# Feed-forward of a one-core DeltaNet layer: windows of 1024 tokens, and w_out in a stage of its own through DRAM

## The chip, the cores and the metric

The kernel runs on one core of a Trainium2 chip. The metric is the device time of one execution in microseconds, as the median of three runs. One further execution, the profiled one, left the trace from which all rows below are read.

## What is computed

One layer: a bidirectional gated DeltaNet mixer over 256 context and 2048 latent tokens of 1024 channels, then a gated feed-forward, then a norm. All inputs are float32. The change touches the feed-forward and what hands over to it:

```python
x_lat = x_lat + mod_l[2] * y_lat
h_lat = modulate(rms_norm(x_lat, norm2_g[i]), mod_l[3], mod_l[4])
x_lat = x_lat + mod_l[5] * conv_glu(h_lat, ...)
return rms_norm(x_lat, final_norm_g)

def conv_glu(h, w_in, conv_w, conv_b, w_out):       # 2 x 2816 inner channels
    val, gate = jnp.split(h @ w_in, 2, axis=-1)
    gate = dw_conv(gate, conv_w) + conv_b           # 3 taps along the tokens
    return (val * jax.nn.silu(gate)) @ w_out
```

## The kernel before

The program has two phases, whose operations (`Op`s of a `Plan`) are put into an order by a list schedule with rough costs and priorities: mixer first (projections, matrices, scans), then `plan2` (the output projection of the mixer, tile by tile of 128 tokens in `OUT_ORDER`, giving `x1_d` and the normed and transposed `h2_d` in DRAM) and `plan3` (the feed-forward). All transfers are issued on SP's queue, in order.

Every product is done in three matmuls, because a float32 operand is carried as two parts, `hi` and `lo`, that float32r holds: hi·hi, hi·lo, lo·hi (`mm3`, L832 to 836). Making the parts is a step of its own (`form`): ScalarE casts `hi` (L1752), VectorE or GpSimd subtracts it to get `lo` (L1755).

`plan3` works on four windows of 512 tokens (`WINDOWS`). In each, 11 groups follow one another; a group is two times 128 inner channels. Of a group the gate's product and the value's product are each a two by two block product: channels by halves of the contraction by halves of the window's tokens (256, for the gate 258 with a halo). `products3` takes seven products instead of eight (Winograd's), so that sums of blocks of the weights (`raw`, L1834, on GpSimd), of the tokens (`braw`, L1789, on VectorE, once a window) and of the results (`pc`, L1885; `zg`, L1931; `val`, L1962, on VectorE out of PSUM) take the place of the eighth. One product is four times `mm3`: 12 matmuls, with tile name `fps`, stationary `wf`, moving `bf`. Four PSUM banks (tags `zp` and `tr`, two each) hold the products in turn. Then come the taps of the convolution (`facc`, L1948, two on VectorE), SiLU, the product with the value and the parts of the hidden channels (`hid`, GpSimd L1970 and L1978).

The same group is at once multiplied with its 256 rows of `w_out`: the rows are loaded, split (`w`, L2000 and L2003, the latter on VectorE), 48 matmuls of 512 columns (`fy`) make the part of the output of four token tiles, and VectorE adds each half tile out of PSUM to a running sum in SBUF (`ya`, L2027). After the last group the sum is scaled, added to `x1`, normed and stored (`final`, L2050 to L2058; for the last window `rescale` and `finish`, L2072 to L2104).

So `w_in` (22 MB) and `w_out` (11 MB) are read and split once for each of the four windows, 44 groups in all. In the program's order on PE each group is 168 `fps` matmuls and 48 `fy` matmuls.

## Time and profile before

| | us |
|---|---|
| median of 3 runs | 3507.01 (3506.76 to 3510.5) |
| profiled execution, first to last instruction (its span, the only time recorded of it) | 3517.0 |
| PE busy in the span | 3302.4 (94%) |
| VectorE busy | 3017.5 (86%) |
| GpSimd busy | 2533.5 (72%) |
| ScalarE busy | 2016.5 (57%) |

PE is the matmul side of TensorE, PEld its weight loads, DVE VectorE, ACT ScalarE, POOL GpSimd, SP the queue of the transfers. The feed-forward begins at about 2000 us and runs to the end. A matmul's own duration contains the time through the array and overlaps the next one; what a matmul costs in a row of them is the step from one start to the next.

### The profile page before, as it was taken

How to read it: one execution, taken by the hardware profiler on the slowest of the kernel's cores; microseconds unless marked ns; L12 is line 12 of the kernel's file. 1: busy time of each engine (PE TensorE's matmuls, PEld its weight loads, DVE VectorE, ACT ScalarE, POOL GpSimd, SP SyncE). 2: the span in 40 equal slices, each digit the busy share in tenths (PEclk: the TensorE clock that was granted, in tenths of full speed). 3: DMA queues.
4: the chain of work that ended last, by engine and by line, in shares of the span. 5: the costliest groups of instructions: out<-in, count | busy, mean ns of one | idle time of the engine just before them, and what ended most of it. 6: DMA issues, size and time to landing. Idle time of an engine off the chain costs nothing.

```text
span 3517.0 us, 74716 instructions
## 1 busy us (share of the span) xinstructions
PE 3302.4 (94%) x27594; PEld 3027.7 (86%) x27594; DVE 3017.5 (86%) x5574; ACT 2016.5 (57%) x5265; POOL 2533.5 (72%) x2630
## 2 busy tenths in 40 slices
PE   7979999999999999999999889998999899988998
PEld 4969899999899989999977789987899789977997
DVE  6678788888898898886565699999999999999998
ACT  6548666666677777776355454444444444444443
POOL 5347677676777787776555587778887888778876
PEclk8989999999999999999999999999999999999999
DMA  7321132232323232322566533333333333324232
GB/s 247 124 68 54 39 98 78 81 97 75 107 75 96 71 105 68 84 60 77 175 197 199 168 104 106 104 107 126 97 108 97 125 110 101 108 72 146 93 104 90
DMA packets 198309, 373.18 MB, mean 106 GB/s; under 512 B 18865, under 2 KB 103081, under 8 KB 196920
## 3 DMA queue, kind: packets, MB, share of 16 engines
q1 hardware_dynamic: 197944, 368.41, 34.2%
q8 instruction: 217, 3.56, 0.4%
q14 instruction: 148, 1.21, 0.1%
HBM read 316.36 MB, written 51.98 MB: 105 GB/s over the span
## 4 chain that ended last, share of the span: by engine, by line
PE 59%; DVE 22%; issue 6%; POOL 6%; ACT 4%; DMA 3%; SPq 0%; DVEq 0%; ACTq 0%; POOLq 0%
PE zps L834 6%; PE fps L834 5%; PE fps L836 5%; PE fps L835 5%; PE zps L835 5%; PE zps L836 5%; PE fy L834 3%; DVE acc L891 3%; PE fy L835 3%; PE fy L836 3%; PE scps L1248 3%; POOL raw L1834 3%; DVE wf L1755 2%; PE scps L1266 2%; PE scps L1275 2%
## 5 line engine op out<-in xcount | busy, mean ns | idle before, releaser
L834 PE MATMUL fps<-bf,wf 128*128 128x258 f32 (+1 forms) x2464 | 708.5, 288 | 61.6 <-DVE val L1962 27.2
L834 PE MATMUL zps<-hhl,wt 128*128 128x260 f32 (+1 forms) x2176 | 697.5, 321 | 10.5 <-DVE acc L891 6.3
L836 PE MATMUL fps<-bf,wf 128*128 128x258 f32 (+1 forms) x2464 | 701.5, 285 | 1.3 <-DVE wf L1755 1.1
L835 PE MATMUL fps<-bf,wf 128*128 128x258 f32 (+1 forms) x2464 | 701.9, 285 | 0.0
L835 PE MATMUL zps<-hhl,wt 128*128 128x260 f32 (+1 forms) x2176 | 619.4, 285 | 1.9 <-POOL hhl L962 1.9
L836 PE MATMUL zps<-hhl,wt 128*128 128x260 f32 (+1 forms) x2176 | 618.8, 284 | 0.0
L962 POOL TENSOR_TENSOR hhl<-hraw,hhl 128x260 fp32r<-128x260 f32 x568 | 427.7, 774 | 155.0 <-ACT hhl L958 152.7
L834 PEld LDWEIGHTS fps<-bf,wf 128*128 128x128 f32 x2464 | 473.1, 192 | 75.7 <-DVE val L1962 27.8
L1752 ACT CAST wf<-raw 128x512 fp32r<-128x512 f32 x616 | 360.4, 619 | 305.1 <-POOL raw L1834 147.3
L1755 DVE TENSOR_TENSOR wf<-raw,wf 128x512 fp32r<-128x512 f32 x440 | 498.3, 1144 | 26.3 <-ACT wf L1752 24.5
L835 PEld LDWEIGHTS fps<-bf,wf 128*128 128x128 f32 x2464 | 473.4, 192 | 1.7
L836 PEld LDWEIGHTS fps<-bf,wf 128*128 128x128 f32 x2464 | 472.8, 192 | 2.1 <-DVE wf L1755 2.1
L891 DVE SCALAR_TENSOR_TENSOR acc<-zps,convw,acc 128x256 f32<-128x256 f32 x832 | 398.8, 480 | 60.5 <-ACT acc L889 44.7
L834 PEld LDWEIGHTS zps<-hhl,wt 128*128 128x128 f32 x2176 | 417.6, 192 | 19.7 <-issue 10.5
L835 PEld LDWEIGHTS zps<-hhl,wt 128*128 128x128 f32 x2176 | 418.3, 192 | 2.4 <-POOL hhl L962 2.3
L836 PEld LDWEIGHTS zps<-hhl,wt 128*128 128x128 f32 x2176 | 414.9, 191 | 0.1
L1834 POOL TENSOR_TENSOR raw<-raw 128x512 f32<-128x512 f32 x176 | 288.0, 1636 | 160.9 <-DVE wf L1755 145.0
L1152 POOL TENSOR_TENSOR ct<-U,cst_lm 128x256 f16<-128x256 f16 x432 | 303.5, 724 | 66.6 <-PE inv L1159 54.3
L1182 ACT CAST yz<-inv 128x256 f16<-128x256 f32 x864 | 275.4, 380 | 85.9 <-PE inv L1176 83.4
L1755 POOL TENSOR_TENSOR wf<-raw,wf 128x512 fp32r<-128x512 f32 x176 | 268.7, 1545 | 76.2 <-ACT wf L1752 75.4
L834 PE MATMUL fy<-w,hid 128*128 128x512 f32 x704 | 282.0, 401 | 30.3 <-DVE ya L2027 27.8
L1834 POOL TENSOR_TENSOR raw<-raw,raw 128x512 f32<-128x512 f32 x176 | 278.6, 1583 | 12.6
(258 smaller groups left out, 8929.7 us busy)
## 6 DMA issues: line engine op xcount, KB each, us to landing
raw<-in_ffn_in SPq DMA_DIRECT2D x176, 512.0 KB
hraw<-hT_d SPq DMA_DIRECT2D x284, 260.0 KB
raw<-in_ffn_out SPq DMA_DIRECT2D x88, 512.0 KB
wmx<-in_w_mod SPq DMA_DIRECT2D x128, 128.0 KB
wt_st<-in_w_qkv SPq DMA_DIRECT2D x24, 512.0 KB
hT_d<-hb SPq DMA_DIRECT2D x36, 260.0 KB
wm<-in_w_mod SPq DMA_DIRECT2D x8, 1024.0 KB
xt<-in_x SPq DMA_DIRECT2D x16, 512.0 KB
```

Of the source, the lines that this page charges most:

```text
L834: mm(out, lh, rh, start=first, stop=False)
L835: mm(out, lh, rl, start=False, stop=False)
L836: mm(out, ll, rh, start=False, stop=last)
L891: nc.vector.scalar_tensor_tensor(acc.t, ps.t[:, k:k + TB], wk, acc.t, ALU.mult, ALU.add)
L962: nc.gpsimd.tensor_tensor(t[:, 1, k], raw[q].t[:, k], t[:, 0, k].bitcast(F32), ALU.subtract)
L1152: nc.gpsimd.tensor_tensor(col_sets(ct, lb, LATE), col_sets(U.t[:, 0], lb, LATE), v3(self.lm[:, li]), ALU.mult)
L1182: nc.scalar.copy(col_sets(yz.t[:, k], lb, sets), v3(ps.t[:, k]))
L1248: nc.tensor.matmul(ps.t[:, k, :], blk.t[:, ci, k, :], S.t, start=True, stop=True)
L1266: nc.tensor.matmul(ps.t[:, 2, :], pz.t[:, ci, 0, :], r.t if S is not None else blk.t[:, ci, 3, :], start=True, stop=True)
L1752: nc.scalar.copy(f.t[:, 0], src())
L1755: (nc.vector if eng == "DVE" else nc.gpsimd).tensor_tensor(f.t[:, 1], src(), f.t[:, 0].bitcast(F32), ALU.subtract)
L1834: return pl.op("POOL", 1.25, lambda: nc.gpsimd.tensor_tensor(part(*out), part(*a), part(*b), op), deps, prio, uses=[raw[k] for k in {out[0 ...
```

## The change

- **Two stages.** `ffn_window` now runs over two windows of 1024 tokens and ends with the hidden channels, unsplit, in DRAM (`hid_d`). `ffn_out` follows: for each half of the 1024 output columns and each block of 512 tokens (the last two blocks 256) it loads the hidden channels, splits them, and sums all 22 times 128 channels in PSUM, in one bank for each token tile, on two sets of four banks in turn.
- **Wider products.** The halves of a window's tokens are 512, so an `fps` matmul has 512 columns, and there are no halos: the convolution runs over the window, and three columns are carried to the next (`carry`).
- **Sums of token blocks through DRAM.** `combine` makes T1 to T4 and stores them in `comb_d`; `tokens` loads blocks and sums in halves of the contraction and splits them. For the second window `combine` runs during the first.
- **Who splits.** All `lo` parts of `w_in` are VectorE's (before, two of seven were GpSimd's). The `lo` parts of the hidden channels move from GpSimd to VectorE and are made twice, once for each half of the columns; those of `w_out` are made once instead of four times, half of them on GpSimd. The `ya` sums are gone; in their place stand, once, a scaling out of PSUM and a sum (`half_out`, `finish_out`), with the first half of the rows kept in `y_d`.
- `OUT_ORDER` has the blocks of the first 1024 tokens before the last three.

What operations there are (built program): `fps` matmuls 7392 before, 3696 now; `fy` 2112 and 2112. On VectorE `wf` 440 of 512 columns before, 462 of 512 and 44 of 256 now (308 for `w_in`, the rest hidden channels), `w` 176 to 10 of 1024 columns (now `bf<-raw`), `ya` 320 to none, results out of PSUM 616 of 256 or 258 to 308 of 512. On GpSimd `raw` 352 to 176, `wf` 176 and `hid` 88 to none.

Core of the diff (removed comments and what follows from the new tile names left out):

```diff
-HT = TB + 2
+WB = 512
...
-OUT_ORDER = [4, 5, 3, 6, 2, 1, 7, 8]
+OUT_ORDER = [4, 5, 3, 2, 1, 6, 7, 8]
...
-WINDOWS = [1, 0, 2, 3]
-FIRST_SLOTS = {"bf": 7, "raw3": 2, "wf": 1}
+SLOTS3 = {
+    "braw": (4, 0, 0), "bf": (5, 7, 2), "raw3": (2, 0, 2), "wf": (4, 0, 3), "pc": (0, 3, 0), "big3": (0, 2, 4), "st3": (0, 0, 4),
+}
...
+    def combine(self, w, prio):
...
+            def less(k, r, a, b, deps, p=p, bufs=bufs):
+                x = pl.op("DVE", 1.15, lambda: nc.vector.tensor_tensor(
+                    bufs[r].t, bufs[a].t, bufs[b].t, ALU.subtract), deps, prio, uses=[bufs[x] for x in {r, a, b}])
+                s = self.comb_done[k, p] = pl.op("SP", 1.5, lambda: nc.sync.dma_start(
+                    self.comb_d[w][k][:, 2 * p:2 * p + 2, :], bufs[r].t), [x], prio, uses=[bufs[r]])
+                return x, s
+            l = [load(0, 0, 0), load(1, 0, 1), load(2, 1, 1), load(3, 1, 0)]
+            t1, s1 = less(0, 0, 1, 0, l[:2])
+            t3, _ = less(2, 1, 2, 1, [t1, l[2]])
+            t2, _ = less(1, 0, 2, 0, [t3, s1])
+            less(3, 3, 3, 0, [t2, l[3]])
+        self.combine(w, prio - (0 if w == 0 else 900))
+        done = dict(self.comb_done)
+        def form(src, deps, eng):
+            r = Buf("braw")
...
+        def block(q, j, eng="DVE"):
+            blk = 2 * w + j
+            deps = [self.h2_done[4 * blk + c] for c in range(4)]
+            return [form(self.h2_d[blk][:, 4 * q + 2 * p:4 * q + 2 * p + 2, :], deps, eng) for p in range(2)]
...
+        b11, b21, t1, t2 = block(0, 0), block(1, 0), comb(0, "POOL"), comb(1)
+        t3, b22, t4 = comb(2, "POOL"), block(1, 1), comb(3)
+        return b11, b21, b22, t4, t1, t2, t3
...
+        f3 = form(1, 0, [s3], "DVE")
-        f4 = form(0, 1, [s4], "POOL")
-        f3 = form(1, 0, [s3], "POOL")
+        f4 = form(0, 1, [s4], "DVE")
...
+            def mms(p):
+                if p == 0:
+                    acc.t = self.pp.tile([P, WB], F32, name="fps", tag=acc.tag, bufs=2)
+                for k in range(2):
+                    kk = 2 * p + k
                     self.mm3(
-                        cols(acc), w.t[:, 0, k, :], w.t[:, 1, k, :], x.t[:, 0, k, toks], x.t[:, 1, k, toks], k == 0, k == 3
+                        acc.t, w.t[:, 0, kk, :], w.t[:, 1, kk, :], x[p].t[:, 0, k, :], x[p].t[:, 1, k, :], kk == 0, kk == 3
                     )
-            acc.done = pl.op(
-                "PE", 12 * (n + 8) / 2400, mms, [w.done, x.done, self.last_out], prio, alloc=[acc], uses=[w, x]
-            )
+            a = self.last_prod
+            for p in range(2):
+                a = pl.op(
+                    "PE", 1.37, lambda p=p: mms(p), [w.done, x[p].done, self.last_out, a], prio,
+                    alloc=[acc] if p == 0 else [], uses=[w, x[p]] + [acc] * p,
+                )
+            acc.done = self.last_prod = a
             return acc
...
-    def ffn_window(self, k, w):
+    def ffn_window(self, w):
+        N = 2 * WB
...
+        n = N + 1 if w else N - 1
+        t0 = N - 1 if w else 0
...
+                def times(f=f):
+                    nc.gpsimd.tensor_tensor(v_[f].t[:, :n], v_[f].t[:, :n], a_[f].t[:, :n], ALU.mult)
+                def store(f=f):
+                    nc.sync.dma_start(self.hid_d[g][:, f, t0:t0 + n], v_[f].t[:, :n])
+                e = pl.op("POOL", 0.1, ends, vals[f], prio, uses=[v_[f]])
+                a = pl.op("POOL", 2.4, times, [e, acts[f]], prio, uses=[v_[f], a_[f]])
+                self.hid_done.setdefault(w, []).append(pl.op("SP", 1.5, store, [a], prio, uses=[v_[f]]))
+        for g in range(NF // 2):
+            hidden(g, base + 20 * g)
...
-                    hid.t = self.pools3[2].tile([P, 2, 2 * TB], F32R, name="hid", bufs=self.NHID)
-                    nc.scalar.copy(hid.t[:, 0], v_[f].t)
...
-                w2.done = pl.op("DVE", 0.61, lambda w2=w2, part=part: TT(
-                    w2.t[:, 1], part(), w2.t[:, 0].bitcast(F32), ALU.subtract), [a], prio, uses=[st, w2])
...
-                    TT(accs[t].t[:, ns], ps.t, accs[t].t[:, ns], ALU.add)
...
-        ng = NF // 2
-        for g in range(ng + 1):
...
+    def ffn_out(self):
...
+        for half in range(2):
+            ns = slice(half * WB, (half + 1) * WB)
+            W = []
+            blocks = [[0, 1, 2, 3], [4, 5, 6, 7], [8, 9, 10, 11]] + ([[12, 13], [14, 15]] if half else [[12, 13, 14, 15]])
+            for i, ts in enumerate(blocks):
+                prio = base + 1000 * half + 100 * i
+                t0, nt = ts[0] * P, len(ts)
+                ps = [Buf((("inv", "inv", "sc", "sc"), ("zp", "zp", "tr", "tr"))[n_acc % 2][t]) for t in range(nt)]
+                n_acc += 1
+                a = None
+                for j in range(nj):
+                    p = prio + j - 25
+                    if i == 0:
+                        raw, l = self.load3(
+                            "raw3", [P, 2, WB], self.i["ffn_out"][2 * j:2 * j + 2, :, ns].rearrange("f p c -> p f c"), [], p
+                        )
+                        W.append(self.form(lambda raw=raw: raw.t, [2, WB], raw, [l], p, "bf", "DVE" if j % 2 else "POOL"))
+                    deps = self.hid_done[0] + (self.hid_done[1] if t0 + nt * P > 2 * WB - 1 else [])
+                    raw, l = self.load3("raw3", [P, 2, nt * P], self.hid_d[j][:, :, t0:t0 + nt * P], deps, p)
+                    hids = [
+                        self.form(lambda raw=raw, f=f: raw.t[:, f], [nt * P], raw, [l], p, "wf", "DVE") for f in range(2)
+                    ]
...
+                    for f in range(2):
+                        first = j == 0 and f == 0
+                        a = pl.op(
+                            "PE", 0.684 * nt, lambda f=f, mms=mms: mms(f), [a, W[j].done, hids[f].done], prio + j,
+                            alloc=ps if first else [], uses=[W[j], hids[f]] + ([] if first else ps),
+                        )
...
+                for t, c in enumerate(ts):
+                    if half == 0:
+                        y_done[c] = self.half_out(prio + 20, c, ps[t], a, near, m5, m5_done)
+                    else:
+                        self.finish_out(prio + 20, c, ps[t], a, near, m5, fg, junk, [m5_done, fg_done, new_junk], y_done[c], i > 2)
...
+    def half_out(self, prio, c, ps, done, near, m5, m5_done):
...
+        a = pl.op("DVE", 0.67, lambda: nc.vector.tensor_tensor(
+            row.t[:, :WB], ps.t, m5.t[:, :WB], ALU.mult), [l, done, m5_done], prio, uses=[row, ps, m5])
+        a = pl.op("POOL", 1.25, lambda: nc.gpsimd.tensor_tensor(
+            row.t[:, :WB], row.t[:, :WB], row.t[:, WB:], ALU.add), [a], prio, uses=[row])
...
+    def finish_out(self, prio, c, ps, done, near, m5, fg, junk, ready, y_done, late):
...
+        eng, add = ("DVE", nc.vector) if late else ("POOL", nc.gpsimd)
...
+        a = pl.op("DVE", 0.67, scaled, [done, *ready], prio, alloc=[tmp], uses=[ps, m5])
+        a = pl.op(eng, 0.61 if late else 1.25, lambda: add.tensor_tensor(
+            row.t[:, WB:], row.t[:, WB:], tmp.t, ALU.add), [a, l], prio, uses=[row, tmp])
+        s1 = pl.op("ACT", 0.6, lambda: square(1), [a, s0], prio, uses=[row, junk, st])
...
+        for k in range(2):
+            s = slice(k * WB, (k + 1) * WB)
+            a = pl.op("DVE", 0.67, lambda s=s: nc.vector.scalar_tensor_tensor(
+                row.t[:, s], row.t[:, s], st.t[:, 2:3], fg.t[:, s], ALU.mult, ALU.mult), [r], prio, uses=[st, row, fg])
+            pl.op("SP", 0.8, lambda s=s: nc.sync.dma_start(self.o[c * P:(c + 1) * P, s], row.t[:, s]), [a], prio, uses=[row])
```

PE, where products and `fy` meet. Before, in the middle of a window; `fps` has 256 columns, and the next group's products come 48 `fy` later:

```order
L834 MATMUL fps<-bf_37086,wf_38099 128x256
L835 MATMUL fps<-bf_37086,wf_38099 128x256
L836 MATMUL fps<-bf_37086,wf_38099 128x256
L834 MATMUL fy<-w_37991,hid 128x512
L835 MATMUL fy<-w_37991,hid 128x512
L836 MATMUL fy<-w_37991,hid 128x512
```

The change, at the only place where they meet (`wf` is then a split of hidden channels, `bf` one of `w_out`):

```order
L839 MATMUL fps<-bf_36593,wf_39501 128x512
L840 MATMUL fps<-bf_36593,wf_39501 128x512
L841 MATMUL fps<-bf_36593,wf_39501 128x512
L839 MATMUL fy<-bf_39594,wf_39625 128x512
L840 MATMUL fy<-bf_39594,wf_39625 128x512
L841 MATMUL fy<-bf_39594,wf_39625 128x512
```

The `fy` have moved from 44 places to the end: all 3696 `fps` stand in front of all 2112 `fy`, and only the output projection's last transposes stand among the first `fps`.

VectorE, from the value's products of a group to the next group, before (`raw` is the float32 load, `wf` its split, `pc` and `val` results out of PSUM, `w` splits of `w_out`, `ya` the running sums):

```order
L1962 TENSOR_TENSOR val<-fps,pc 128x256 x2
L1755 TENSOR_TENSOR wf_44595<-raw_44382,wf_44595 128x512
L1755 TENSOR_TENSOR wf_44597<-raw_44382,wf_44597 128x512
L1962 TENSOR_TENSOR val<-fps,pc 128x256
L1755 TENSOR_TENSOR wf_44611<-raw_44420,wf_44611 128x512
L2027 TENSOR_TENSOR ya<-fy,ya 128x512 x4
L2003 TENSOR_TENSOR w_44656<-raw_44443,w_44656 128x512
L2003 TENSOR_TENSOR w_44659<-raw_44601,w_44659 128x512
L2027 TENSOR_TENSOR ya<-fy,ya 128x512 x4
```

The change, over one set of seven products of the first window (`big` takes the results):

```order
L1957 TENSOR_TENSOR big_36115<-fps,pc_36095 128x512
L1755 TENSOR_TENSOR wf_36124<-raw_35930,wf_36124 128x512
L1904 TENSOR_TENSOR pc_36142<-fps,pc_36095 128x512
L1904 TENSOR_TENSOR pc_36146<-fps,pc_36142 128x512
L1755 TENSOR_TENSOR wf_36144<-raw_35930,wf_36144 128x512
L1904 TENSOR_TENSOR pc_36166<-fps,pc_36142 128x512
L1957 TENSOR_TENSOR big_36168<-fps,pc_36166 128x512
L1755 TENSOR_TENSOR wf_36164<-raw_35908,wf_36164 128x512
L1957 TENSOR_TENSOR big_36115<-fps,pc_36146 128x512
```

The `w` splits and `ya` sums are gone from between the products; at most one split stands between two results, and each piece is twice as wide against twice the columns of a product.

SP, from the last tiles of the output projection on (`x_d` and `h_d` are that projection's stores), before:

```order
L1776 DMA braw<-h_d_70 128x4x256
L1550 DMA x_32924<-in_x 128x1024
L1675 DMA h_d_75<-h_32938 1024x1x128
L1633 DMA x_d_98<-x_32796 128x1024
L1550 DMA x_33023<-in_x 128x1024
L1675 DMA h_d_75<-h_33036 1024x1x128
L1633 DMA x_d_99<-x_32924 128x1024
```

The change, at the same place:

```order
L1821 DMA braw_33077<-h_d_69 128x1024
L1674 DMA h_d_72<-h_33061 1024x1x128
L1821 DMA braw_33092<-h_d_69 128x1024
L1821 DMA braw_33106<-h_d_69 128x1024
L1635 DMA x_d_130<-x_32928 128x1024
L1821 DMA braw_33136<-comb_d_84 128x1024
L1821 DMA braw_33151<-comb_d_84 128x1024
L1821 DMA braw_33169<-comb_d_85 128x1024
```

From the `h2_d` store that completes the first window to the last token part, 30 transfers of 512 KB (8 loads and 8 stores of `combine`, 14 loads of `tokens`) stand among the projection's own, where 4 stood before.

## Rows read from the trace of the kernel before

**Rows 1.** Page part 2, the span in 40 slices (digits: tenths busy).
```profile
PE   7979999999999999999999889998999899988998
DVE  6678788888898898886565699999999999999998
```

**Rows 2.** Stretches: busy us (xcount) of PE, PEld, DVE, ACT, POOL; clock, DMA.
```profile
2300.00:2500.00 200.00, 175.93 (x1155) 160.54 (x1154) 189.43 (x225) 92.74 (x161) 162.36 (x101) 0.95 0.37 117
2900.00:3100.00 200.00, 200.00 (x1410) 187.81 (x1408) 190.22 (x258) 97.91 (x167) 157.11 (x101) 1.00 0.35 104
2000.00:3517.00 1517.00, 1412.18 (x9513) 1299.90 (x9511) 1444.76 (x1823) 713.40 (x1241) 1211.10 (x768) 0.98 0.34 107
```

**Rows 3.** PE's waits, 2000 to 3517 us: total, times, longest.
```profile
PE fy L834 <- DVE ya L2027: 27.8, 18, 5.0
PE fps L834 <- DVE val L1962: 27.2, 7, 5.1
PE fps L834 <- DVE zg L1931: 20.6, 14, 3.4
```

**Rows 4.** Timeline of PE, one whole group: start us, us, engine, line, operation.
```profile
2914.84 0.39 PE L834 MATMUL fy<-w,hid 128*128 128x512 f32 x1
...
2925.81 0.28 PE L834 MATMUL fps<-bf,wf 128*128 128x258 f32 x1
...
2935.88 0.28 PE L834 MATMUL fps<-bf,wf 128*128 128x256 f32 x1
...
2945.96 0.40 PE L834 MATMUL fy<-w,hid 128*128 128x512 f32 x1
```

**Rows 5.** Timeline of PE, first and last of 23 `yps` products in a row.
```profile
1961.29 0.39 PE L835 MATMUL yps<-wo,og 128*128 128x512 f32 x1
...
1966.42 0.40 PE L836 MATMUL yps<-wo,og 128*128 128x512 f32 x1
```

**Rows 6.** Timeline of PE, the first feed-forward product and the first regular `fy`.
```profile
2000.03 0.28 PE L834 MATMUL fps<-bf,wf 128*128 128x258 f32 x1
...
2093.99 0.39 PE L834 MATMUL fy<-w,hid 128*128 128x512 f32 x1
```

**Rows 7.** Timeline of PE, one change of window, first and last `fy` run.
```profile
2343.45 0.39 PE L834 MATMUL fy<-w,hid 128*128 128x512 f32 x1
...
2504.22 0.39 PE L834 MATMUL fy<-w,hid 128*128 128x512 f32 x1
```

**Rows 8.** Timeline, PE's last product and VectorE's last piece.
```profile
3507.00 0.39 PE L836 MATMUL fy<-w,hid 128*128 128x512 f32 x1
...
3511.23 2.74 DVE L2102 SCALAR_TENSOR_TENSOR ya<-ya,st,fg 128x512 f32<-128x512 f32 x4 [0.35 <-POOL st L2098]
```

**Rows 9.** Groups by line and shape: xcount, busy us, mean ns, idle before.
```profile
L1755 DVE TENSOR_TENSOR wf<-raw,wf 128x512 fp32r<-128x512 f32 x439 | 497.6, 1145 | 26.3 <-ACT wf L1752 24.5
L1834 POOL TENSOR_TENSOR raw<-raw 128x512 f32<-128x512 f32 x176 | 288.0, 1636 | 160.9 <-DVE wf L1755 145.0 <-DVE st L2053 7.8 <-issue 1.3
L1948 DVE SCALAR_TENSOR_TENSOR facc<-zg,fcw,facc 128x512 f32<-128x512 f32 x176 | 211.9, 1222 | 4.8 <-ACT facc L1945 3.1
L2027 DVE TENSOR_TENSOR ya<-fy,ya 128x512 f32<-128x512 f32 x320 | 200.9, 676 | 7.2 <-PE fy L836 7.0
L1755 DVE TENSOR_TENSOR bf<-braw,bf 128x1032 fp32r<-128x1032 f32 x20 | 35.0, 1748 | 0.8 <-ACT bf L1752 0.8
```

**Rows 10.** Line views: ns of one, least/median/most.
```profile
L1755 DVE TENSOR_TENSOR wf<-raw,wf x440: 672/920/2878, 1780.5 to 3465.6; 128x512 fp32r<-128x512 f32 x147
L1834 POOL TENSOR_TENSOR raw<-raw x176: 1277/1628/2182, 2002.2 to 3463.1; 128x512 f32<-128x512 f32 x176
L1948 DVE SCALAR_TENSOR_TENSOR facc<-zg,fcw,facc x176: 732/1072/1791, 2016.0 to 3474.6; 128x512 f32<-128x512 f32 x176
```

**Rows 11.** Stretches, columns as in rows 2: output projection; the busiest transfers.
```profile
1900.00:2000.00 100.00, 91.98 (x434) 74.67 (x433) 62.30 (x105) 45.46 (x127) 49.07 (x46) 0.97 0.56 170
2430.00:2440.00 10.00, 7.30 (x32) 5.35 (x30) 9.96 (x12) 5.20 (x10) 8.62 (x8) 1.00 0.80 285
```

More of the change, by code (lines that the diff above doesn't have):

```diff
@@ L220, in order @@
                 continue
-            assert events, "the slots do not suffice"
+            assert events, "the slots do not suffice: " + "; ".join(
+                f"{e} {o.prio} {[b.tag for b in o.allocs]} {[b.tag for b in o.uses]}"
+                for e in engines for o in pending[e]
+            )
             t, n = heapq.heappop(events)
@@ L229, in order @@
                     self.slots[b.tag].append((b.slot, o.eng, t))
+            for tag, k in o.opens:
+                self.slots[tag].append((k, None, 0.0))
             for q in o.next:
@@ L1707, in open_a @@
             nc.sync.dma_start(T["fcw"], self.i["ffn_conv"])
+            T["carry"] = self.pools3[0].tile([P, NF, 3], F32, name="carry", bufs=1)
         def open_b():
@@ L1809, in channels @@
+        return b11, b21, b22, t4, t1, t2, t3
     def channels(self, g, t, prio):
         nc, pl = self.nc, self.plan
[L1812 to L1824 removed]
+        raw, loaded = zip(*[
+            self.load3("raw3", [P, KT, P], self.i["ffn_in"][2 * g + k, t], [], prio) for k in range(2)
+        ])
@@ L1920, in hidden @@
         def hidden(g, prio):
             fcw = lambda f, k: T["fcw"][:, 2 * g + f, k:k + 1]
-            zg, a_, v_ = ([Buf(n) for _ in range(2)] for n in ("zg", "facc", "val"))
+            carry = lambda f, a, b: T["carry"][:, 2 * g + f, a:b]
+            zg, a_, v_ = ([Buf("big3") for _ in range(2)] for _ in range(3))
             A = self.channels(g, 1, prio - 25)
             made = [[], []]
-            def gate_put(f, j):
-                def put(x, y):
-                    if not zg[f].t:
-                        new(zg[f], 2 * HT)
-                    TT(zg[f].t[:, j * HT:(j + 1) * HT], x, y, ALU.add)
-                return put, [zg[f]] if j == f else [], [] if j == f else [zg[f]]
@@ L2060, in rescale @@
-        def rescale(t, prio, late):
-            ya, x1 = accs[t], Buf("raw3")
-            c = 4 * w + t
-            def load():
-                self.new3(x1, [P, D])
-                nc.sync.dma_start(x1.t, self.x1_d[c])
-            l = pl.op("SP", 1.5, load, [self.x1_done[c], late], prio, alloc=[x1])
-            for n in range(2):
-                ns = slice(n * 512, (n + 1) * 512)
-                a = pl.op("POOL", 1.25, lambda ns=ns: nc.gpsimd.tensor_tensor(
-                    ya.t[:, ns], ya.t[:, ns], T["m5"][:, ns], ALU.mult), [acc_done[t][n], self.m5_done], prio, uses=[ya])
-                acc_done[t][n] = pl.op("DVE", 0.61, lambda ns=ns: TT(
-                    ya.t[:, ns], ya.t[:, ns], x1.t[:, ns], ALU.add), [a, l], prio, uses=[ya, x1])
@@ L2107, in ffn_window @@
-        ng = NF // 2
-        prev = None
-        for g in range(ng + 1):
-            prio = base + 20 * g
-            hids = hidden(g, prio) if g < ng else None
-            if prev:
-                last = k == len(WINDOWS) - 1 and g == ng
-                ws = [out_weights(2 * g - 2 + f, prio - 18, last) for f in range(2)]
-                late = [d[0] for d in acc_done]
-                if last:
-                    for t in range(4):
-                        rescale(t, prio - 16, before[t])
-                before = late
-                halves = [(n, t) for n in range(2) for t in range(4)]
-                for n, t in sorted(halves, key=lambda x: x[1]) if last else halves:
-                    add(g - 1, prev, ws, n, t, prio + self.ADD + t * last)
-                if g == ng:
-                    for t in range(4):
-                        if last:
-                            finish(t, prio + self.ADD + 4 + t)
-                        else:
-                            final(t, prio + self.FINAL, late[t])
-            prev = hids
+            self.products3(V, B, prio, block_put(v_, v0), vals)
```

381 lines of the change are left out of this document (164 added, 217 removed).

## Prediction

> **What bounds the kernel now.** I read the page by slices first, then the stretches, PE's waits and PE's timeline. The change leaves everything ahead of the feed-forward as it is, apart from the order of the output projection's blocks, so the stage from 2000 us to the end is what counts. There VectorE is at 9 tenths in every slice and PE at 8 to 9 [rows 1]. The stretches part two regimes [rows 2]: in the middle of a window PE is busy all the time at the full clock (200.00 of 200 us, clock 1.00) with VectorE at 95%; around a change of window PE falls to 176 of 200 us and the granted clock to 0.95, VectorE still at 95%. PE's waits name VectorE each time: `ya`, `val` and `zg` are 75.6 us together [rows 3]. So PE sets the pace in the steady part, and VectorE, which has nothing to spare there, sets it wherever a window brings extra work.
>
> PE's price for each kind of product comes from one whole group [rows 4]: 48 `fy` of 512 columns take 2925.81 - 2914.84 = 10.97 us, **0.2285 us** each; 168 `fps` of 258 and 256 columns take 2945.96 - 2925.81 = 20.15 us, **0.1199 us** each; the group 31.12 us. The 44 groups would be 1369 us; the stage has 1517, so 148 us are lost. By the order on PE, 504 `fps`, 48 `fy` and 0.9 us of transposes lie between the first product and the first regular `fy`; they are worth 72 us and took 93.96 [rows 6]: 22 lost at the start. Over one change of window 192 `fy` and 672 `fps` are worth 43.9 + 80.6 = 124.5 us and took 160.77 [rows 7]: 36 lost, three times. From the last matmul to the end of the span are 10 us [rows 8]. That is 22 + 109 + 10 = 141 of the 148.
>
> **The change part by part.** *Products.* Half as many `fps`, twice as wide. A 512-column matmul between weight loads stands in the trace as `fy`, in the same stage and form: 0.2285 us, against two of the narrow ones 0.2398. 3696 x 0.2285 = 844.5 us (before 7392 x 0.1199 = 886). The 2112 `fy` stay: 482.6 us. Together **1327 us** if nothing waits. The output projection's `yps`, of 512 columns too, go at 5.13 / 22 = 0.2332 us [rows 5]; by it the `fps` would be 17 us more. I take `fy`, the stage's own.
>
> *VectorE in the first stage.* A new group has 14 splits `wf` of 512 columns, 14 results out of PSUM of 512 and 4 taps of about 1024. At the least durations [rows 10] that is 14 x 0.672 + 14 x 0.676 (the `ya` mean, also out of PSUM) + 8 x 0.732 = 24.7 us; at the means of before [rows 9] 14 x 1.145 + 9.5 + 8 x 1.222 = 35.3 us. PE needs 168 x 0.2285 = 38.4 us. The splits and taps read two SBUF tensors and spread from 0.67 to 2.9 us, while `ya` has 0.676 on average: the spread comes with GpSimd's work, busy 1211 of 1517 us, 0.80 [rows 2]. A new group has for GpSimd 8 combinations and 4 halves of the product with the value, 12 x 1.636 = 19.6 us of 38.4, 0.51. In proportion VectorE stands at 24.7 + 10.6 x 0.51 / 0.80 = 31.5 us, 82% of the group. So PE sets the pace, and VectorE has 7 us a group to catch up with. Of the sums and splits of `w_out`, 496 pieces before, 10 (wider) are left on VectorE; that is where the room comes from.
>
> The Trainium skill speaks against this room (page "SBUF — State Buffer", section "Who interferes with whom"): a VectorE instruction with two SBUF inputs and a GpSimd one that reads SBUF exclude each other for a whole instruction. If VectorE stood still for all of GpSimd's work, it would have 24.7 + 12 x 1.277 = 40.0 us a group, over PE's 38.4. The trace so far bears out only a part of it, since pieces out of PSUM run beside GpSimd at 0.676 us; the full case is a rival below, with its own mechanism.
>
> *Start.* From 4 transfers the token parts go to 30 of 0.524 MB, 15.7 MB, within about 70 us of output projection. That projection alone keeps the transfers at a share of 0.56 [rows 11]; at the best stretch, 285 GB/s at 0.80, the new ones need 55 us x 0.80 = 44 us of the 16 engines, and 0.56 x 70 + 44 = 83 us do not fit into 70. The first parts are needed first, and the last products of the first set give 14 us more, so little of the 13 should show; I add 8 to the 22 lost before: **30 us**, bounds 10 (parts ready early) and 55 (all 30 transfers late, and PE cold again).
>
> *The one change of window left.* Ten `bf` splits of VectorE's at 1.748 us [rows 9] are 17.5 us within two sets of products (38.4 us), beside 31.5: 10.6 us too many. With some 4 us at the lower clock, 1.2 instead of 2.4 GHz, as the changes of before show a granted 0.95: **15 us**; bounds 5 and the 36 of before. Gone are the finals of three windows, and two changes.
>
> *Between the stages.* The first block needs only tokens of the first window, whose hidden channels have long been stored, and its PSUM banks are other ones than the last products'. Left is filling the pipeline: a load, a cast, a split; PE goes from one to the other in the order with nothing between. In the first block of each half two loads of 0.524 MB are wanted per 24 `fy` (5.5 us), 191 GB/s, in four slots `raw3`. **8 us**; bounds 0 and 95 (a rival). VectorE has 2 to 3 pieces per 5.5 us, no bound.
>
> *End.* Two half tiles are scaled, summed, normed and stored after the last matmul, as before: **10 us**.
>
> Sum: 2000 + 1327 + 30 + 15 + 8 + 10 = 3390, 127 us under the span of 3517.0. The profiled execution is 10 us (0.3%) above the median of the runs; taken from the median, **3380 us**.
>
> **The rivals.** *The shared reads bind.* VectorE stands still for the whole of GpSimd's 12 pieces, at their least duration [rows 10]: 24.7 + 12 x 1.277 = 40.0 us instead of PE's 38.4 in each of 22 groups, 36 us, and no room to catch up at the start and the change, some 12 more: 3428. For it: splits up to 2.9 us. Against: with this counting an old group (10 `wf`, 4 `w`, 4 taps, 8 `ya`, 14 narrow results at about 0.415, and 16 pieces of GpSimd's) would have had 23.5 + 16 x 1.277 = 43.9 us and had 31.1. *The second stage waits for its loads.* If the first block of each half gets only the 107 GB/s that this stage shows on average [rows 2], a step takes 9.8 us instead of 5.5: 22 steps, 95 us: 3475. Against: the same queue moved 285 GB/s in a busy stretch [rows 11]. *Slower than before:* a PSUM bank that comes free late. Product 7 of a set takes the bank of product 3, whose result is needed last after product 5; the cover is product 6, 12 x 0.2285 = 2.7 us. If two splits of 2.88 us (the most in rows 10) stood between the two results in VectorE's order, 2 x 2.88 + 2 x 0.676 = 7.1 us, PE would wait 4.4 us in each of 44 sets, 193 us: 3573. It decides the sign from 3 us a set on. Against: in the order at most one split stands there. *`yps` pace* gives 3397, within the forecast's range. That the change does not do what it says is excluded by the order: the `fps` and `fy` counts and shapes are as described.
>
> **How the numbers follow.** Forecast with either pace 0.73 (its own range 3350 to 3415), shared reads 0.11, late loads 0.10, late bank 0.06. With the low bounds of the terms (10, 5, 0 and 10 us) the time would be 3342; I take 3350, since all at once is unlikely. The high end is 3440: it takes in the shared reads and leaves out the late loads and the late bank, 0.16. Measuring this kernel tells about 0.2% (7 us) from no change. Faster 0.94, same 0.01, slower 0.05.
>
> **What would show it.** Right: `fps` of 512 columns in steps of 0.2285 us, PE at 100% and clock 1.00 within windows, VectorE at 80 to 85% there, one dip at the change and a short one between the stages, `fy` in steps of 0.2285 to the end. Wrong: regular PE waits for results out of PSUM in the middle of a window (shared reads or late bank, told apart by VectorE being full or not), PE waiting for `wf` or `bf` with transfers ahead of it in the second stage, or a dip of over 50 us near 2000 us.

## The result and the profile after

The changed kernel takes **3364.86 us** (median of 4 runs, 3358.7 to 3366.54), the kernel before 3508.52 us beside it: ratio 0.9584, 95% interval 0.9571 to 0.9598, **143.7 us less**. The forecast was 3380, with a range of 3350 to 3440. The profiled execution is one of the four runs, 3358.7 us with a span of 3357.0, 6 us under their median; that of before lay 10 us above its own. The two profiles side by side therefore show 160 us, of which 16 belong to neither kernel.

The page by slices: busy tenths of PE and VectorE and the granted clock, 40 slices of 84 us, to be held against [rows 1].

```profile
PE   7979999999999999999999999999999999999998
...
DVE  6778788888898988888566578666766666523534
...
PEclk8999999999999999999999999999999999999999
```

From slice 26 on VectorE has 6 or 7 tenths and from slice 35 on, in which the second stage begins, 2 to 5, where it had 9. The stretches (PE, PEld, VectorE, ScalarE, GpSimd busy with their counts, then clock, DMA share, GB/s): the start, the middle of the first window, the change of window, the hand-over between the stages at 2859.9, and the second stage.

```profile
2000.00:2050.00 50.00, 43.72 (x181) 34.79 (x180) 45.91 (x49) 20.14 (x28) 28.01 (x20) 0.93 0.64 226
...
2100.00:2400.00 300.00, 300.00 (x1302) 244.23 (x1301) 189.24 (x246) 105.48 (x152) 143.48 (x125) 1.00 0.25 81
...
2400.00:2450.00 50.00, 41.05 (x168) 32.30 (x167) 40.01 (x42) 26.61 (x33) 30.55 (x18) 0.90 0.60 198
...
2850.00:2900.00 50.00, 50.00 (x219) 40.73 (x218) 30.23 (x29) 19.45 (x28) 19.46 (x9) 1.00 0.65 210
2900.00:3100.00 200.00, 200.00 (x869) 162.93 (x868) 66.48 (x87) 48.29 (x76) 22.68 (x15) 1.00 0.44 142
```

PE is full at the full clock everywhere but in two dips. Where the middle of a window of before had VectorE at 95% [rows 2], it now has 189.24 of 300 us, 63%. All that PE waits for from the start of the feed-forward to the end (us in total, times, longest), where [rows 3] named 75.6 us:

```profile
PE fps L839 <- ACT wf L1752: 7.1, 1, 7.1
PE fps L839 <- DVE big L1957: 5.0, 1, 5.0
PE fps L839 <- DVE pc L1904: 2.4, 2, 1.3
PE fps L841 <- DVE wf L1755: 1.1, 2, 0.7
```

PE's timeline at the first product, at the hand-over and at the last product (start, us, engine, line, operation), as [rows 6] and [rows 8] gave it:

```profile
1985.62 0.39 PE L839 MATMUL fps<-bf,wf 128*128 128x512 f32 x1
...
2859.63 0.39 PE L841 MATMUL fps<-bf,wf 128*128 128x512 f32 x1
2859.86 0.39 PE L839 MATMUL fy<-bf,wf 128*128 128x512 f32 x1
...
3346.23 0.39 PE L841 MATMUL fy<-bf,wf 128*128 128x512 f32 x1
```

From these: 874.2 us of products and 486.6 us of `fy`; the second stage follows the first with no gap, and 10.5 us follow the last product. At the steps of the middle of a window, 300 / 1302 = 0.2304 us, the 3696 products are 852 us; 22 are lost, 10 at the start (waits of 5.0, 1.3 and 0.4 us, transposes and products at the lower clock) and 12 at the change (7.1, 1.2 and 0.7 us and the lower clock).

### The profile page after: what moved, and what is told of

It reads as the page before. It is cut to its first block, busy times and chain, and to the rows that moved or that the text cites. A ratio compares the mean times of both kernels' runs of the same rounds, so it can differ in the third digit from the quotient of the medians.

```text
span 3357.0 us, 65714 instructions
## 1 busy us (share of the span) xinstructions
PE 3228.9 (96%) x23898; PEld 2815.0 (84%) x23898; DVE 2380.9 (71%) x4797; ACT 1785.7 (53%) x4773; POOL 1823.7 (54%) x2248
## 4 chain that ended last, share of the span: by engine, by line
PE 76%; DVE 14%; ACT 3%; DMA 3%; POOL 2%; issue 2%; SPq 0%; DVEq 0%; POOLq 0%; ACTq 0%
PE fps L841 8%; PE fps L839 8%; PE fps L840 8%; PE zps L839 6%; PE zps L840 5%; PE zps L841 5%; PE fy L840 5%; PE fy L841 5%; PE fy L839 5%; DVE acc L896 4%; PE scps L1253 3%; PE scps L1271 2%; PE scps L1280 2%; PE gqps L1093 2%; DVE blk L911 1%
## 5 line engine op out<-in xcount | busy, mean ns | idle before, releaser
L1752 ACT CAST wf<-raw 128x512 fp32r<-128x512 f32 (+1 forms) x506 | 302.0, 601 | 733.8 <-PE fps L841 292.4
L1755 DVE TENSOR_TENSOR wf<-raw,wf 128x512 fp32r<-128x512 f32 (+1 forms) x506 | 402.9, 803 | 361.7 <-ACT wf L1752 352.8
L839 PE MATMUL fps<-bf,wf 128*128 128x512 f32 x1232 | 486.1, 395 | 14.6 <-ACT wf L1752 7.1
L841 PE MATMUL fps<-bf,wf 128*128 128x512 f32 x1232 | 485.6, 394 | 1.1 <-DVE wf L1755 1.1
L840 PE MATMUL fps<-bf,wf 128*128 128x512 f32 x1232 | 485.2, 394 | 0.0
L1850 POOL TENSOR_TENSOR raw<-raw 128x512 f32<-128x512 f32 x88 | 116.5, 1324 | 362.6 <-DVE wf L1755 354.2
L839 PEld LDWEIGHTS fps<-bf,wf 128*128 128x128 f32 x1232 | 232.4, 189 | 68.7 <-ACT wf L1752 7.5
L841 PEld LDWEIGHTS fps<-bf,wf 128*128 128x128 f32 x1232 | 232.2, 188 | 55.4 <-DVE wf L1755 2.4
L840 PEld LDWEIGHTS fps<-bf,wf 128*128 128x128 f32 x1232 | 232.3, 189 | 53.1 <-DVE bf L1755 0.3
L840 PE MATMUL fy<-bf,wf 128*128 128x512 f32 x704 | 276.4, 393 | 0.0
L841 PE MATMUL fy<-bf,wf 128*128 128x512 f32 x704 | 276.4, 393 | 0.0
L839 PE MATMUL fy<-bf,wf 128*128 128x512 f32 x704 | 276.3, 392 | 0.0
## 6 DMA issues: line engine op xcount, KB each, us to landing
wmx<-in_w_mod SPq DMA_DIRECT2D x128, 128.0 KB
```

What stands on the lines that cost most here:

```text
L839: mm(out, lh, rh, start=first, stop=False)
L840: mm(out, lh, rl, start=False, stop=False)
L841: mm(out, ll, rh, start=False, stop=last)
L1752: nc.scalar.copy(f.t[:, 0], src())
L1755: (nc.vector if eng == "DVE" else nc.gpsimd).tensor_tensor(f.t[:, 1], src(), f.t[:, 0].bitcast(F32), ALU.subtract)
L1850: return pl.op("POOL", 1.25, lambda: nc.gpsimd.tensor_tensor(part(*out), part(*a), part(*b), op), deps, prio, uses=[raw[k] for k in {out[0 ...
```

## Experiments

Each states its time against the kernel before on the same chip in the same batch. "More" or "less" than the new kernel is the difference of ratios times 3510 us; single differences of under 7 us are not told from nothing.

**1. What the width is worth.** The new kernel with 256-column products:

```diff
-    self.mm3(acc.t, w.t[:, 0, kk, :], w.t[:, 1, kk, :], x[p].t[:, 0, k, :], x[p].t[:, 1, k, :], kk == 0, kk == 3)
+    for s in (slice(0, 256), slice(256, 512)) if p else ():
+        for kk in range(4):
+            xt = x[kk // 2].t[:, :, kk % 2, s]
+            self.mm3(acc.t[:, s], w.t[:, 0, kk, :], w.t[:, 1, kk, :], xt[:, 0], xt[:, 1], kk == 0, kk == 3)
...
```

> The new kernel with each of its products of 512 columns into the hidden channels taken as two of 256, so that only the width is undone. Theory (the width is worth what its steps say): 3696 x (2 x 0.1199 - 0.230) = 36 us more, 3401 us. Rival (the gain comes from the windows and from VectorE's room alone): within 5 us of 3365. Rival (the narrow ones cost more here, because their results are waited for at the banks): over 3430, with waits of PE for VectorE in the middle of a window.

3384.44 us, ratio 0.9642 (0.9628 to 0.9656): **20 us more**. The middle of the window, same columns as above:

```profile
2100.00:2400.00 300.00, 300.00 (x2531) 300.00 (x2530) 181.75 (x241) 104.90 (x150) 139.44 (x120) 1.00 0.25 82
```

300 / 2531 = 0.1185 us, so two narrow ones take 0.2370 where a wide one takes 300 / 1302 = 0.2304: 3696 x 0.0066 = 24 us. PE's weight loads are busy all of the time here, and 244 of 300 us with wide products. The width is worth about 20 us, not the 36 of the theory, since a pair of 256-column products is faster here than the 0.2398 of [rows 4]. The other part is 7392 x (0.1199 - 0.1185) = 10 us, and what makes it stays open. It is not the two neighbouring columns of the gate's products: in [rows 4] 84 products of 258 columns took 10.07 us and 84 of 256 columns 10.08.

**2 to 5. What made the losses around the changes of window.** The prediction put the 109 us there, and part of the 22 at the start, down to a full VectorE. Four versions of the kernel before each take work of a change away. First the taps:

```diff
 def tap(k, f=f, shifted=shifted, acc=acc):
-    nc.vector.scalar_tensor_tensor(acc(), shifted(k), fcw(f, k), acc(), ALU.mult, ALU.add)
+    pass
```

> The kernel before, without the two later taps of the feed-forward's convolution (176 instructions of VectorE, 215 us of its time, are left out and its work is otherwise in the same order). Theory (a full VectorE made the losses around the changes of window): 70 to 110 us less, 3400 to 3440, and VectorE well under 95% in the changes. Rival (the order of transfers and casts made them): at most 20 us less, 3488 or more, with PE waiting for transfers and casts there.

3469.02 us, 0.9881 (0.9864 to 0.9897): **42 us less**, between what the theory and its rival expected. Then the later windows' token parts:

```diff
-        B = self.tokens(w, base - 30)
+        if k == 0:
+            self.B = self.tokens(w, base - 30)
+        B = self.B
```

> The kernel before, with the token parts of the first window used for all four, so that the loads, sums and splits of the three later ones are left out (30 us of VectorE at each change, and 24 transfers). Theory (VectorE, full, sets the losses at the changes, and this is the largest piece of what a change brings): 60 to 100 us less, 3410 to 3450. Rival (the finals of the outgoing window make the losses): under 40 us less, 3470 or more.

3483.41 us, 0.9922 (0.9908 to 0.9937): **27 us less**; it was the largest piece on paper, and the expectation failed. Then the finals (in `final`, the store takes `acc_done[t]` and the operations ahead of it go):

> The kernel before, with the finals of the first three windows left out (the sums are stored as they are; per change 12 us of VectorE, 13 us of GpSimd, 5 us of ScalarE and four loads less). Theory (the losses at a change go with VectorE's extra work there, 12 of 42 us): 36 x 12 / 42 = 10 us a change, 30 us less, 3480. Rival (the finals make the losses): 70 us less or more, 3440. Rival (they lie beside other work, since nothing waits for them): within 7 us of before.

3460.26 us, 0.9863 (0.9848 to 0.9878): **48 us less**, more than its 12 us of VectorE a change. So none of the three alone is the cause, and the work on VectorE does not price them: the finals, the smallest on VectorE, also bring 13 us of GpSimd. Without them PE's order changes too: the 48 `fy` of each of the first two groups of a later window stand together, where the kernel before has them in runs of 12, 6 and 30, and of 6 and 42. Then all three edits together:

> The kernel before, with all three left out at once: the two later taps, the token parts of the later windows, and the finals of the first three windows. Alone they took 42, 27 and 50 us off. Theory (each is a part of the same thing, VectorE's time in the stretches where it is full, so they add up until the losses of 131 us at the start and the changes are gone): 105 to 125 us less, 3385 to 3405, PE at 100% at the changes. Rival (they relieve the same waits, so that the largest alone gives most of it): 50 to 75 us less, 3435 to 3460.

3408.89 us, 0.9697 (0.9676 to 0.9717): **106 us less**, as the theory expected; the three alone add up to 117. The stretch of [rows 2] that held a change, 2300 to 2500, in the kernels without taps, without tokens, without finals, and without all three:

```profile
2300.00:2500.00 200.00, 182.07 (x1215) 166.84 (x1214) 175.01 (x215) 96.90 (x169) 166.28 (x107) 0.97 0.39 122
```
```profile
2300.00:2500.00 200.00, 182.83 (x1195) 168.85 (x1195) 183.55 (x229) 91.27 (x161) 159.44 (x100) 0.96 0.34 106
```
```profile
2300.00:2500.00 200.00, 187.76 (x1253) 171.51 (x1253) 187.97 (x234) 97.23 (x167) 156.91 (x104) 0.98 0.35 111
```
```profile
2300.00:2500.00 200.00, 197.79 (x1361) 183.88 (x1360) 161.50 (x221) 97.74 (x172) 151.64 (x103) 1.00 0.35 111
```

PE goes from 175.93 to 182, 183, 188 and 198 of 200 us. Only the last has no dip, and VectorE at 81%. Counted as in [rows 7], the first change of window, 160.8 us before, takes 150.8, 150.1, 143.2 and 128.0 us in these four, against 124.5 without waits. So 97 of the 106 us came back at the three changes and 7 at the start, where 15 of the 22 stay lost. That the losses go with this work is shown. The taps are VectorE's alone; the other two edits also take away transfers, casts on ScalarE and pieces of GpSimd's, and the finals change PE's order, so the share of VectorE alone is not told apart.

**6. The other side: does VectorE hold anything up now?** The new kernel with its two later taps replaced by `pass` in the same way.

> The new kernel, without the two later taps of the convolution (88 instructions of VectorE, over 100 us of its time, left out). Theory (PE's steps are all that counts in the first stage, VectorE has room): 3355 to 3365, and only the waits at the start and at the change may shrink. Rival (VectorE still holds PE up in places that the share of 60% hides): 20 us less or more, under 3345.

3356.88 us, 0.9563 (0.9548 to 0.9577): 7 us less, at the edge of what can be told. In the middle of the window PE was at 300.00 of 300 before and is now, with VectorE at 155.17. The gain is at the start:

```profile
2000.00:2050.00 50.00, 47.32 (x204) 37.66 (x203) 43.62 (x50) 22.31 (x32) 27.02 (x22) 1.00 0.73 257
```

PE has 3.6 us more there, and the clock no longer falls: the 5.0 us wait for `big`, a result that stood behind two taps and a split on VectorE, is 1.4 us. The first group takes 44.1 us instead of 49.0, against 38.7 later on, so about half of what is lost at the start hung on the taps. With 34 us in 300 less on VectorE nothing changed in the middle of the window, and at the change the wait for `wf` is still 7.0 us.

**7. How much room VectorE has.**

```diff
 def lo():
-    (nc.vector if eng == "DVE" else nc.gpsimd).tensor_tensor(
-        f.t[:, 1], src(), f.t[:, 0].bitcast(F32), ALU.subtract)
+    for _ in range(2 if tag == "wf" else 1):
+        (nc.vector if eng == "DVE" else nc.gpsimd).tensor_tensor(
+            f.t[:, 1], src(), f.t[:, 0].bitcast(F32), ALU.subtract)
```

> The new kernel with each split of a weight or a hidden channel into its low part done twice on VectorE, with the same result: 14 x 0.80 = 11 us more in each group of 38.4 us. Theory (VectorE stands at 24 us a group, as its share of 62% says): 35 us a group, still under PE's, 3365 to 3378. Rival (the prediction's 31.5 us a group): 43 us against 38.4, 22 groups x 4.3 = 95 us more, 3460, with PE waiting for VectorE in every group.

3459.72 us, 0.9853 (0.9838 to 0.9868): **94 us more**. My theory fell. The rival had the time right, in part by luck: PE does wait for VectorE throughout, but its sum starts from 31.5 us a group, where 24.4 are measured, and adds 11, where 15 came. The middle of the window, PE's main wait (from the start of the feed-forward on), and the splits in that stretch (count, busy, mean ns, idle before):

```profile
2100.00:2400.00 300.00, 283.84 (x1204) 226.94 (x1203) 282.59 (x329) 96.51 (x143) 136.40 (x116) 0.99 0.25 75
```
```profile
PE fps L839 <- DVE pc L1905: 65.1, 38, 6.6
```
```profile
L1756 DVE TENSOR_TENSOR wf<-raw,wf 128x512 fp32r<-128x512 f32 x201 | 192.9, 965 | 14.4 <-ACT wf L1752 10.9
```

In that stretch a group takes 168 x 300 / 1204 = 41.9 us, and VectorE is busy for 39.4 of them; in the new kernel it is 168 x 300 / 1302 = 38.7 us, with VectorE busy for 24.4. That is 15 us more, where 14 pieces of 0.672 us are 9.4 on paper. GpSimd does the same work, but the splits are 965 ns on average instead of 782. In the new kernel:

```profile
L1755 DVE TENSOR_TENSOR wf<-raw,wf 128x512 fp32r<-128x512 f32 x108 | 84.5, 782 | 43.2 <-ACT wf L1752 42.0
```

All of the loss lies in the first stage, which takes 970.8 us from the first product to the first `fy` instead of 874.2; the second takes 486.4 us in both. So 14 us that were free in a group by VectorE's average share did not hold 14 more pieces.

**8. Room against more GpSimd.**

```diff
 nc.gpsimd.tensor_tensor(part(*out), part(*a), part(*b), op)
+s = self.ffn_t["spare"]
+nc.gpsimd.tensor_tensor(s, s, s, ALU.add)
```

> The new kernel, with one more GpSimd addition of 512 columns, on a spare tile of zeros, behind each of the eight combinations of a group: GpSimd 48% goes to about 78%, and VectorE gets no work. The prediction let VectorE's splits grow in proportion to GpSimd's share: 0.67 + 0.47 x 0.78 / 0.80 = 1.13 us each, against 0.80 now; VectorE then 75%, PE at 100%, time within 10 us of 3365. Rival (the splits are stretched only by what stands beside them in the chain of preparation, and the share of GpSimd says nothing): 0.80 to 0.95 us each, same time. Rival (the chain of cast, split and combination, longer by 4 x 1.3 us a set, is no longer ahead of PE): PE waits for wf in every group, 20 to 100 us more.

3382.38 us, 0.9618 (0.9586 to 0.9650): some 12 us more, with intervals that touch. The same two views:

```profile
2100.00:2400.00 300.00, 300.00 (x1303) 244.26 (x1302) 213.31 (x250) 105.65 (x156) 210.04 (x188) 1.00 0.24 78
```
```profile
L1757 DVE TENSOR_TENSOR wf<-raw,wf 128x512 fp32r<-128x512 f32 x109 | 109.2, 1006 | 52.6 <-ACT wf L1754 52.6
```

GpSimd at 70% instead of 48% lengthens the splits from 782 to 1006 ns and VectorE's share from 63 to 71%. The proportional rule gives 24.7 + 10.6 x 0.70 / 0.80 = 34.0 us a group; measured are 213.31 / 300 x 38.7 = 27.5. The sign of the rule holds, its size doesn't. PE stays full in the middle; the time is lost in longer dips.

**9 and 10. The dip at the change.** In the trace PE waits there for a cast of weights that stands on ScalarE behind the cast of a token part, and that waits for its load, the last but one of `comb_d`. On SP that load stood behind two stores of hidden channels. ScalarE and SP (the SP rows give the issue):

```profile
2437.41 1.05 ACT L1752 CAST bf<-braw 128x1024 fp32r<-128x1024 f32 x1 [7.29 <-DMA braw<-comb_d]
```
```profile
2427.56 3.80 SPq L2005 DMA_DIRECT2D hid_d<-big  x2
2431.46 1.15 SPq L1821 DMA_DIRECT2D braw<-comb_d  x2
```

Experiment 9 frees GpSimd ahead of these stores (`comb(0, "DVE" if w else "POOL")`, and the same for `comb(2)`):

> The new kernel, with the four splits of token sums that GpSimd makes for the second window moved to VectorE. In the trace these hold GpSimd for 6 us just ahead of the last group's products with the value, whose stores stand on SP ahead of the last loads of token sums. Theory (this chain, stores ahead of loads, makes the 7.1 us wait of PE for a split at the change): the wait shrinks to 1 to 2 us, the whole is 5 to 10 us shorter, about 3357. Rival (VectorE, busy 40 of 50 us there, makes the dip): no gain or up to 6 us more, 3365 to 3371.

3364.88 us, 0.9587 (0.9573 to 0.9602): nothing. PE's wait for `wf` is 4.3 us instead of 7.1, but the waits for splits grow from 1.1 to 2.9. Experiment 10 takes the stores out of SP's order (`nc.gpsimd.dma_start` in place of `nc.sync.dma_start`, as an operation of GpSimd's):

> The new kernel, with the stores of the hidden channels issued from GpSimd, right behind the product that they wait for, instead of from SP. Theory (the last loads of token sums stand behind two such stores in SP's order): PE's 7.1 us wait at the change goes, 7 to 12 us less, 3353 to 3358. Rival (the casts on ScalarE wait for transfers that are late anyway, DMA share 0.60 there): within 3 us of 3365. If issuing costs GpSimd much, it shows as a higher share of GpSimd and not in the time, as GpSimd stands at 50%.

3367.22 us, 0.9594 (0.9578 to 0.9610): nothing, and the wait stays at 7.6 us. My theory, that the stores hold the loads up, fell as well. In this version's trace the loads of `comb_d` are issued when VectorE's split of the part two before them ends, at 2434.95 + 1.25 = 2436.20:

```profile
2436.22 3.81 SPq L1821 DMA_DIRECT2D braw<-comb_d  x2
```
```profile
2434.95 1.25 DVE L1755 TENSOR_TENSOR bf<-braw,bf 128x1024 fp32r<-128x1024 f32 x1 [1.49 <-ACT bf L1752]
```

My reading is that load, cast, split and the slot that comes free follow each other through four slots of `braw`, so that taking one link away leaves the next. It is read from the trace and no run shows it; experiment 12 has a fifth slot, and its dip is longer.

**11. The order of the output projection's blocks**, which the prediction named without a price.

```diff
-OUT_ORDER = [4, 5, 3, 2, 1, 6, 7, 8]
+OUT_ORDER = [4, 5, 3, 6, 2, 1, 7, 8]
```

> The new kernel with the old order of the output projection's blocks (4, 5, 3, 6, 2, 1, 7, 8), in which the first window's tokens are complete one block of 256 tokens later, so that the 30 transfers, the sums and the splits of the first window have some 35 us less ahead of the first product. Theory (the new order is what kept the start at a loss of 12 us): 10 to 35 us more, 3375 to 3400, in waits of PE for token parts at 2000 us. Rival (there is enough time either way): within 5 us of 3365.

3382.11 us, 0.9624 (0.9605 to 0.9643): **14 us more**. PE at the start, and two of its waits:

```profile
2000.00:2050.00 50.00, 39.16 (x158) 28.97 (x159) 44.42 (x43) 26.70 (x34) 24.99 (x17) 1.00 0.68 241
```
```profile
PE fps L840 <- DVE bf L1755: 5.1, 5, 1.4
...
PE fps L840 <- POOL bf L1755: 5.0, 4, 1.7
```

With the old order PE waits for token parts; with the new one no wait of PE's is for one.

**12. A version meant to be faster**: edit 9, and

```diff
-"braw": (4, 0, 0), ... "wf": (4, 0, 3)
+"braw": (4, 0, 1), ... "wf": (4, 0, 2)
...
 deps = [self.b_load] + [self.h2_done[4 * blk + c] for c in range(4)]
+     + (self.hid_done[0][8:9] if w else [])
```

> A version meant to be faster: the sums of the second window's token blocks (8 VectorE sums, 16 transfers) wait for the fifth group instead of standing in the start, where VectorE is busy 46 of 50 us; the second window's four GpSimd splits of token sums are on VectorE; one slot more for token parts in SBUF and one fewer for splits of weights. Theory (VectorE's queue makes the 5 us wait at the start, the chain of token parts through four slots the 7 us wait at the change): 5 to 15 us less than 3365, 3350 to 3360. Rival (waits move along to the next link, as in the two earlier attempts at the change): within 4 us of 3365.

3372.95 us, 0.9597 (0.9573 to 0.9620): not faster. The start has 48.08 of 50 us of PE instead of 43.72, but 2200 to 2300, where the sums now stand, has lost 6: 93.97 of 100. The dip at the change is longer as well: the first group of the second window takes 54.9 us instead of 48.9, with a wait of 9.5 us for a split on VectorE, in the stretch that has 41.05 of 50 us of PE in the new kernel:

```profile
2400.00:2450.00 50.00, 38.01 (x148) 30.02 (x147) 42.83 (x42) 26.23 (x32) 18.70 (x15) 0.86 0.56 189
```

Behind the sums is a stretch with nothing special in it, here in this version and in the new kernel:

```profile
2300.00:2400.00 100.00, 100.00 (x436) 81.57 (x435) 74.10 (x83) 33.62 (x49) 49.13 (x42) 1.00 0.28 85
```
```profile
2300.00:2400.00 100.00, 100.00 (x435) 81.41 (x434) 62.23 (x81) 33.57 (x49) 49.84 (x43) 1.00 0.26 85
```

Nearly the same instructions in the same numbers, GpSimd as busy, and VectorE is at 74% instead of 62%. What differs is the slots, six for splits instead of seven and five for token parts instead of four, and with them when pieces meet; no run takes these apart.

## Why the prediction was right, and where its terms were off

| term | predicted, us | measured, us |
|---|---|---|
| first product | 2000 | 1985.6 |
| 3696 products | 844.5 | 852 |
| 2112 `fy` | 482.6 | 486.6 |
| start | 30 (10 to 55) | 10 |
| change of window | 15 (5 to 36) | 12 |
| between the stages | 8 (0 to 95) | 0 |
| end | 10 | 10.5 |
| span | 3390 | 3357 |

**The mechanism held.** The forecast rested on two claims. That PE's steps set the time once VectorE has room: PE is full at clock 1.00 in both windows and in all of the second stage. That VectorE's extra work made the losses at the changes: taking it out of the kernel before gives back 106 us (experiment 5), 97 of them at the changes, where the prediction counted 109, and the new kernel recovers 131 - 22 = 109 with the start. How much of the 97 is VectorE's alone is not shown; the taps, which are, gave 31 there. With about 20 us for the width, 10 for the faster steps of 256 columns and 14 for the blocks' order the parts come to 150, against 143.7 measured; the 7 us of experiment 5 that lie at the start may be counted twice in it, and the intervals of the single experiments are 5 us and more wide.

That the time came as near as 15 us is in part luck: the stage's terms were 31 us too high at the start, the change and the hand-over, and 12 us too low in the steps.

**Steps of products: off by 12 us.** 0.2285 became 0.2304 in the first stage and 486.6 / 2112 = 0.2304 in the second, between `fy` of [rows 4] and `yps` of [rows 5]. The gain of the products as predicted, 886 - 844.5 = 41.5 us, came out as 34, and a third of it is not width, as experiment 1 shows. Why the step is longer by 1.9 ns than that of `fy` before stays open.

**First product: 14.4 us early.** Some 11 us of it lie ahead of everything that the change touches: the last product of the scans, `scps`, is at 1709.3 us and was at 1720.1. The traces of the other runs have it anywhere from 1709.7 to 1722.9 us, in versions of either kernel. So this is the distance of single executions, which the prediction had taken off at the end, from span to median.

**Start: 30 predicted, 10 measured.** The step that failed is that 83 us of transfers do not fit into 70. From 1950 to 2000 us the transfers ran at 301 GB/s with a share of 0.88, more than the 285 and 0.80 of [rows 11], and no wait of PE's was ended by one:

```profile
1950.00:2000.00 50.00, 48.07 (x227) 38.65 (x226) 35.52 (x45) 24.63 (x40) 17.34 (x12) 1.00 0.88 301
```

The order of blocks gave 14 us (experiment 11), and it had no term. Of the 10 us that are lost, 6.7 are PE's waits for VectorE, and about half went with the taps (experiment 6).

**VectorE in a group: 31.5 us predicted, 24.4 measured**, the lower bound of 24.7 in practice. The step that failed is the growth of its pieces in proportion to GpSimd's share: at 0.48 the splits are 782 ns, at 0.70 they are 1006 (experiment 8), and with GpSimd no busier they are 965 and 1069 (experiments 7 and 12). An average hides how they grow. Least, median and longest of a split from 2100 to 2400 us, in the new kernel and in experiment 12:

```profile
L1755 DVE TENSOR_TENSOR wf<-raw,wf x108: 679/693/1157, 2101.9 to 2398.6; 128x512 fp32r<-128x512 f32 x108
```
```profile
L1755 DVE TENSOR_TENSOR wf<-raw,wf x106: 672/692/2574, 2100.0 to 2399.6; 128x512 fp32r<-128x512 f32 x106
```

Half of the splits take within 20 ns of the least in both. What differs is how many take over 1 us, 18 of 108 and 43 of 106; all 18 and 42 of the 43 begin while a piece of GpSimd's runs. What decides how many meet is not shown. In the new kernel GpSimd often waits for VectorE, so that the two take turns: its combinations `raw<-raw` had 135.4 us of idle time ahead of them in 300 us, 134.1 ended by a split of VectorE's. But in experiment 12 it is 154.5 us, and the splits are longer, so turns alone do not explain it.

```profile
L1850 POOL TENSOR_TENSOR raw<-raw 128x512 f32<-128x512 f32 x32 | 41.4, 1294 | 135.4 <-DVE wf L1755 134.1
```
```profile
L1850 POOL TENSOR_TENSOR raw<-raw 128x512 f32<-128x512 f32 x30 | 40.6, 1354 | 155.7 <-DVE wf L1755 154.5
```

**Change: 15 predicted, 12 measured, near by luck.** The "10.6 us too many" on VectorE were not it: VectorE has 40.01 of 50 us there, and the taps' time taken off it left the wait at 7.0 us (experiment 6). PE's 7.1 us wait ended with a cast behind that of a token part, for whose load ScalarE had waited 7.3. That the cause is the chain through the slots of `braw` is argued; experiments 9 and 10 show two links that are not it alone, and which would have to go stays open.

**Between the stages: 8 predicted, none measured.** The loads, casts and splits of the second stage were made while the last products ran.

**The rivals.** The shared reads did not bind: 24.4 and not 40.0 us a group, PE at 300.00 of 300. The trace bears out a part of it: from 2100 to 2400 us pieces with a PSUM input stay at 684 to 692 ns on average in every version of the new kernel, while splits go from 745 to 1069. The Trainium skill (page "SBUF — State Buffer", section "Who interferes with whom") states that a VectorE instruction with at most one SBUF input, outside the 2-port modes, which `tensor_tensor` does not have, does not contend with GpSimd. The trace agrees for the pieces out of PSUM. Two SBUF inputs do not always make a piece longer, though: the taps have them and stay at 1280 to 1281 ns on average. The rival's count had let all of VectorE's work stand still. Experiment 7 shows that the way to a full VectorE is short, 14 splits more. Late loads: none, the first blocks of the second stage moved 210 GB/s with PE full. The late bank: no regular wait in the middle of a window.

## What to carry to other kernels

Test what a stall is worth by leaving work of the stretch around it out of the old kernel, one kind alone and all together: three pieces that took 42, 27 and 48 us off alone took 106 off together, while their instruction times ranked them otherwise. A second engine's average share says neither how much room it has nor how long its pieces will be; 14 of 38.7 us free were gone after 14 pieces that take 0.67 us at the least, and with other slots the same pieces beside the same share of GpSimd took 12 points more of VectorE. Look at the median and the longest piece too. Where a dip looks like a chain of slots, one link less can leave the wait as it was, so count the links before trying.

## What the runs showed of the hardware

Two 256-column products with weight loads of their own take 0.2370 us (experiment 1), one of 512 takes 0.2304 in the new kernel: doubling the width gained 3%. In the versions of the new kernel VectorE's splits with two SBUF inputs range from 745 to 1069 ns on average with the same shape from 2100 to 2400 us, and the two furthest apart, experiments 1 and 12, have GpSimd busy for 46% of the time in both (in experiment 12 the stretch also holds the eight sums). The DMA queues moved 301 GB/s beside PE at 48.07 of 50 us and at the full clock.
